# Two groups of key blocks per value burst in the attention heads, and block scores between the query products

## The chip, the cores and the metric

The program runs on one core of one Trainium2 chip. The metric is the device time of one execution in microseconds (us), the median of several runs. The engines are TensorE (PE for its matmuls, PEld for its weight loads), VectorE (DVE), ScalarE (ACT), GpSimd (POOL), and SyncE (SP), which issues most transfers. Each engine works through its own queue in order. About 0.2% of the time, 3.7 us, is what a measurement of this kernel can tell from no change.

## The reference

Two decoder layers over 512 tokens of width 1024. Each layer is: feed-forward (gated, inner width 2816), normalisation, attention, normalisation, feed-forward, normalisation. The attention of the first layer is a latent attention of 12 heads. The second layer attends to keys and values that are made once from the output of the first, in three branches. Every layer also has four memory heads that attend to a memory of 256 rows; their output stands beside that of the 12 heads in one output projection.

```python
# first layer, 12 heads, causal
s = einsum('bhqd,bhkd->bhqk', qb, k) * scale
p = masked_softmax(s, key_pos <= tq)
o = einsum('bhqk,bhkd->bqhd', p, v)
# second layer: 31 compressed keys, selected blocks, window, each with its gate
s_c = einsum('bghqd,bgnd->bghqn', qb, kc) * scale - m * dist_c
p_c = masked_softmax(s_c, cmp_end <= tq)
o   = gb[..., 0:1] * o_c + gb[..., 1:2] * o_s + gb[..., 2:3] * o_w
# both layers
o_mem = memory_attention(q_mem, mem, w_mem_kv[layer])
mix = concatenate([o_tok, o_mem], -1) @ w_out[layer]
```

With 512 tokens there are 8 blocks of 64, and 16 may be selected, so every block is; the window covers all tokens as well. The selected and the window branch are both a causal attention with a distance bias, over two sets of keys and values.

## The kernel before

Tokens and features are cut into tiles of 128 rows. Products of 32-bit data are made of parts: a value is split into a high and a low part (`split`: one ACT and one DVE instruction), and `mm3` and `feature_major` sum three products of parts. Transposed tiles and the products with values stay plain 32-bit; each such value product appears in the trace as two matmul records.

**The order of the work.** The kernel is written for a framework that takes the instructions in program order, estimates when each would be ready, and lays down a fixed order for each engine; an instruction whose inputs come late may so be placed behind others of its engine that were written after it. Buffers are tiles of pools with a number of slots per tag; a new tile waits until the slot's last reader is done. On chip, each queue is strictly in the order laid down.

**The heads.** `pipeline` (both attentions) walks through the score steps: a head has four, one per query block i = 3, 2, 1, 0. A step issues the score matmuls (L351 to L353 and L883 in the first attention, L1191 and L1193 in the second), a maximum on DVE (L884, L1196), exponentials on ACT (L885, L1198); after two blocks, POOL multiplies the rows with the reciprocal of their sums (L891, L1205) into the tile `pp`. After each score step, one step of `others` (next queries and keys) and one of `all_values` run. When the scores are done, `run_all` goes on with values and the first products of the output projection.

**Values.** The heads' values are done for a pair of heads. `GROUPS_J` cuts the lower triangle of 4 x 4 key and query blocks into three groups: key block 0 with 512 query columns, key block 1 with 384, key blocks 2 and 3 with 256 and 128. The second attention has two branches, so six groups. The schedule `SCHED` is a tuple of steps. The word `a0` is `flipped` for group 0 and the first head of the pair: transposes on PE (L618) into one of two PSUM tiles `tb`, and a copy (L621) on ACT or DVE into a tile `pt`, two slots per head. `b0` is the same for the second head. `x0` is the group's products with the values (L646): per key block one matmul for each head, 64 columns wide, the first head in the lower half of the PSUM tile `o` and the second in the upper half. After the last group, the second attention adds the product with the compressed values (L1220), and `put_mix` splits `o` into the tile that the output projection reads. The last step of a pair and the first step of the next run in the same step of the pipeline. `memory_values` does the same for the two pairs of memory heads (products at L704), one of two key blocks at a time.

**The query products of the second attention.** `nsa_in` makes the gates and memory queries, then six query products (`feature_major`, each 128 features for 512 tokens); `q_out` splits a product into `qf`. Between the first ones run the eight steps of `memory_scores`, in PSUM banks 5 to 7. Then come the scores against the compressed keys: `block_scores` (six matmuls from two entries of `qf`, an ACT copy into `ct`) and `block_softmax` (a load of the bias `al`, four transposes L1069, the softmax L1073 to L1084 on DVE with one ACT exponential), for two of three groups of heads, in iterations 3 to 5; the third group is done later, within the heads. The results are in the tile `pc`, which is transposed and read (L1167) in the heads. `query` issues the loads for a pair's query tiles (L1053 on POOL, L1054 and L1055 on SP). PSUM has eight banks; when the heads begin, the banks 0 to 4 become their score tiles, 5 and 6 the two `tb` tiles and 7 the tile `o`.

Of the kernel before, what the change touches and what calls it, by code (L numbers as in the profile page):

```python
# [9 lines left out]
F32 = mybir.dt.float32  # L10
# [7 lines left out]
P = 128  # L18
T = 512
D = 1024  # L20
NT = 4
# [3 lines left out]
NPAIR = 6  # L25
# [79 lines left out]
def tile_trunk(ctx: ExitStack, tc, a: dict, out):  # L105
    nc = tc.nc
# [70 lines left out]
    def unit(name, idx, look):  # L177
        assert order[W.pos][:2] == (name, tuple(idx)), (order[W.pos], name, idx)
        if W.done <= W.pos:
            prep()  # L180
        ahead(look)
        W.pos += 1
        return W.ready.pop(W.pos - 1)
# [51 lines left out]
    def bank(i):  # L235
        i %= 8
        return (PS.left if i < 5 else PS.right).tile([P, 512], F32, tag=f"b{i}", name="bank")
# [22 lines left out]
    def otile():  # L260
        return PS.right.tile([P, 512], F32, tag="o", name="o")
# [93 lines left out]
    def feature_major(w, ps, c0, c1):  # L355

        hi, lo = w
        if c1 - c0 > 256:
            feature_major(w, ps, c0, c0 + 256)
            feature_major(w, ps, c0 + 256, c1)  # L360
            return
        for k in range(NKT):
            nc.tensor.matmul(ps[:, c0:c1], lhsT=hi[:, k * P:(k + 1) * P], rhs=F.xhi[:, k, c0:c1],  # L363
                             start=k == 0, stop=False)
            nc.tensor.matmul(ps[:, c0:c1], lhsT=hi[:, k * P:(k + 1) * P], rhs=F.xlo[:, k, c0:c1],  # L365
                             start=False, stop=False)
        for k in range(NKT):
            nc.tensor.matmul(ps[:, c0:c1], lhsT=lo[:, k * P:(k + 1) * P], rhs=F.xhi[:, k, c0:c1],  # L368
                             start=False, stop=k == NKT - 1)
# [244 lines left out]
    def flipped(pget, js, par, eng):  # L614

        tb = ttile()
        for c, (j, i) in enumerate(js):
            nc.tensor.transpose(tb[:, c * P:(c + 1) * P], pget(i, j), ident)  # L618
        n = len(js) * P
        pt = F.pt.tile([P, T], F32, tag=f"pt{par}", name="pt", bufs=2)  # L620
        (nc.scalar.copy if eng else nc.vector.tensor_copy)(pt[:, :n], tb[:, :n])  # L621
        return pt
# [70 lines left out]
    def memory_values():  # L693
        for pr in range(2):
            F.o = otile()
            for j in range(2):
                pts = []
                for e in range(2):
                    pts.append(flipped(lambda i, j: F.pm[2 * pr + e][:, i, j * P:(j + 1) * P],
                                       [(j, i) for i in range(NT)], e, e))  # L700
                yield
                for e in range(2):
                    c = 512 + j * 256 + (2 * pr + e) * 64
                    nc.tensor.matmul(F.o[64 * e:64 * e + 64, :], lhsT=F.kv[:, c:c + 64], rhs=pts[e],  # L704
                                     start=j == 0, stop=j == 1)
            put_mix(6 + pr)

# [92 lines left out]
    def mla_heads(cT):  # L800
# [93 lines left out]
        def values(pr):  # L894
# [8 lines left out]

            yield from causal_values(SCHED, 1, pget, v, True, lambda g, e: (g + e) % 2)
            put_mix(pr)

        SCHED = ("a0", "b0", "", "x0 a1", "b1", "x1 a2", "b2", "", "x2")

        def scores():
            yield from memory_scores(lambda n: stile())  # L910
# [146 lines left out]
    def block_scores(g, qf, ps, pool, tag, bufs=1):  # L1057

        for v in range(2):
            mm3(ps, S.kc[:, v, 0], S.kc[:, v, 1], qf[:, 2 * g + v, 0], qf[:, 2 * g + v, 1], v == 0, v == 1)  # L1060
        ct = pool.tile([P, T], F32, tag=tag, name="ct", bufs=bufs)
        nc.scalar.copy(ct, ps)
        return ct

    def block_softmax(pc, g, ct, gt, tb, pool, tag, tp, bufs=1):
        al = pool.tile([P, T], F32, tag=tag, name="al", bufs=bufs)
        nc.sync.dma_start(al, a["alc"][g])
        for i in range(NT):
            nc.tensor.transpose(tb[:, i * P:(i + 1) * P], ct[:, i * P:(i + 1) * P], ident)  # L1069
        sc = pc.rearrange("p t s n -> p (t s) n")  # L1070
        m = tp.tile([P, 16], F32, name="m")
        r = tp.tile([P, NT, 2, 2], F32, name="r")
        nc.vector.tensor_tensor(pc.rearrange("p t s n -> p (t s n)"), tb, al, op=ALU.add)  # L1073
        nc.vector.tensor_reduce(m, sc, axis=AX.X, op=ALU.max, negate=True)
        nc.vector.tensor_tensor(sc, sc, m[:, :, None].to_broadcast([P, 16, 32]), op=ALU.add)
        nc.scalar.activation(pc, pc, AF.Exp)
        rf = r.rearrange("p t v e -> p (t v e)")
        nc.vector.tensor_reduce(rf, sc, axis=AX.X, op=ALU.add)
        gv = gt.rearrange("p t (e h b) -> p t h e b", e=2, h=NPAIR)[:, :, 2 * g:2 * g + 2, :, 0]
        nc.vector.tensor_scalar(rf, rf, 1e-30, None, op0=ALU.max)  # L1080
        nc.vector.tensor_tensor(r, r, gv, op=ALU.mult)
        nc.vector.reciprocal(rf, rf)
        nc.vector.tensor_scalar(rf[:, 0:4], rf[:, 0:4], valid, None, op0=ALU.mult)
        nc.vector.tensor_tensor(sc, sc, rf[:, :, None].to_broadcast([P, 16, 32]), op=ALU.mult)  # L1084

    def nsa_in(gt, qf):
        tst, tp = right_pool("ntmp", 2)
        ws = [unit("wgq", (i,), 5 - i) for i in range(3)]
        wq = [unit("wq", (i,), 2 - i) for i in range(3)]

        def gates_qmem(t):
            ps = bank(t)
            q = slice(t * P, (t + 1) * P)
            for k in range(NKT):
                hi, lo = ws[k // 3]
                c = slice(k % 3 * 292, k % 3 * 292 + 292)
                mm3(ps[:, 0:292], F.xhi[:, k, q], F.xlo[:, k, q], hi[:, c], lo[:, c], k == 0, k == NKT - 1)
            nc.scalar.activation(gt[:, t, :], ps[:, 0:36], AF.Exp, scale=-1.0)
            c = F.xp.tile([P, 256], F32, tag=("g", "b")[t % 2], name="c")
            nc.scalar.copy(c, ps[:, 36:292])  # L1100
            return c

        def qmem(t, c):
            q = slice(t * P, (t + 1) * P)
            pt = bank(4 + t)
            for b in range(2):
                nc.tensor.transpose(pt[:, b * P:(b + 1) * P], c[:, b * P:(b + 1) * P], ident)
            for b in range(2):
                split(F.qm[b][:, 0, q], F.qm[b][:, 1, q], pt[:, b * P:(b + 1) * P], scale=0.125)

        def q_out(i, p):
            split(qf[:, i, 0, :], qf[:, i, 1, :], p, scale=0.125)

        c = [gates_qmem(0), gates_qmem(1)]
        qmem(0, c[0])
        pq = [bank(i) for i in (0, 1, 4)]
        feature_major(wq[0], pq[0], 0, 256)
        qmem(1, c[1])
        for i in (1, 2):
            feature_major(wq[i], pq[i], 0, 256)  # L1120
        c = [gates_qmem(2), gates_qmem(3)]
        qmem(2, c[0])
        late = [c[1]]
        nc.vector.tensor_scalar(gt, gt, 1.0, None, op0=ALU.add)
        scores = memory_scores(lambda n: bank(5 + n % 3))
        for i in range(3):
            feature_major(wq[i], pq[i], 256, 512)
            if late:
                qmem(3, late.pop())
            q_out(i, pq[i])  # L1130
            next(scores)
            next(scores)
        for i in range(3, NPAIR):
            p = bank(i - 1)
            feature_major(unit("wq", (i,), 2), p, 0, T)
            q_out(i, p)
            if i == 3:
                for _ in scores:
                    pass
                F.qx = [[mix_tile(5), mix_tile(4)]]  # L1140
                F.pc = F.mp.tile([P, 2, NT, 4, 32], F32, tag="mx2", name="pc")
                query(0, qf, F.qx[0])
            else:
                block_softmax(F.pc[:, i - 4], i - 4, ct, gt, bank(6), F.xp, f"x{i - 2}", tp)
            if i < 5:
                ct = block_scores(i - 3, qf, bank(5), F.xp, "g")
        tst.close()

    def nsa_heads(gt, qf):
# [58 lines left out]
        def values(pr):  # L1208
# [9 lines left out]

            yield from causal_values(SCHED, 2, pget, v, False, lambda g, e: (g + e) % 2)
            nc.tensor.matmul(F.o, lhsT=S.vc[:, pr % 2], rhs=ptc[:, pr // 2], start=False, stop=True)  # L1220
            put_mix(pr)

        SCHED = ("a0 b0", "a1 x0", "b1 a2", "x1 b2", "x2 a3 b3", "a4 x3", "b4 a5", "x4 b5", "x5")

        def first():
            yield from memory_values()
# [65 lines left out]
    pc = bank(7)  # L1292
# [30 lines left out]
    ast, ap = right_pool("ain0")  # L1323
# [21 lines left out]
    ast, ap = right_pool("ain1")  # L1345
    qf = ap.tile([P, NPAIR, 2, T], F32R, name="qf")
    gt = ap.tile([P, NT, 36], F32, name="gt")
    nsa_in(gt, qf)
    close_f()
    for side in ("left", "right"):  # L1350
# [162 lines left out]
```

## Time and profile before

| what | value |
|---|---|
| median of 3 runs | 1870.72 us (1868.49 to 1872.56) |
| the profiled execution | 1869.39 us, its span 1867.5 us |
| mean granted TensorE clock | 0.997 |
| heads of the first attention, with their start | about 405 to 521 us |
| query products of the second attention | about 1306 to 1347 us |
| heads of the second attention | 1347 to 1483 us |

The rows of the profile have the form "start, duration, engine, line, operation, out<-in, shape, count", with times in us from the start of the span; idle time of the engine ahead of a row, and what ended it, stands in brackets. Consecutive instructions of one line are one row. In a table by windows each engine has its busy time and, in brackets, its instructions; then follow the granted clock of TensorE as a share of full speed, the busy share of the DMA engines and their rate. The rows that carry the argument are shown with the prediction.

### The profile page before, as it was taken

How to read it: one execution, taken by the hardware profiler on the slowest of the kernel's cores; microseconds unless marked ns; L12 is line 12 of the kernel's file. 1: busy time of each engine (PE TensorE's matmuls, PEld its weight loads, DVE VectorE, ACT ScalarE, POOL GpSimd, SP SyncE). 2: the span in 40 equal slices, each digit the busy share in tenths (PEclk: the TensorE clock that was granted, in tenths of full speed). 3: DMA queues.
4: the chain of work that ended last, by engine and by line, in shares of the span. 5: the costliest groups of instructions: out<-in, count | busy, mean ns of one | idle time of the engine just before them, and what ended most of it. 6: DMA issues, size and time to landing. Idle time of an engine off the chain costs nothing.

```text
span 1867.5 us, 31922 instructions
## 1 busy us (share of the span) xinstructions
PE 1842.7 (99%) x12776; PEld 1651.6 (88%) x12776; DVE 1465.6 (78%) x2362; ACT 869.4 (47%) x1435; POOL 164.3 (9%) x185
## 2 busy tenths in 40 slices
PE   9999999999999999999999999999999999999998
PEld 8899899896679899899998998998956689999997
DVE  8798789757668789788897987987677378888887
ACT  6344345456545345334653443444566345434432
POOL 0000000025500000000100000001265100000000
PEclk9999999999999999999999999999999999999999
DMA  6333335531134234234333323343321224323322
GB/s 241 112 114 111 116 105 157 173 102 35 57 113 136 80 102 136 80 102 147 130 127 104 125 91 103 112 138 140 108 46 28 98 77 143 103 90 114 115 81 77
DMA packets 59701, 203.86 MB, mean 109 GB/s; under 512 B 6944, under 2 KB 7216, under 8 KB 59552
## 3 DMA queue, kind: packets, MB, share of 16 engines
q1 hardware_dynamic: 56848, 194.18, 31.8%
q0 software_dynamic: 2416, 7.11, 1.2%
q8 instruction: 101, 1.65, 0.4%
q10 hardware_dynamic: 288, 0.52, 0.1%
q14 instruction: 48, 0.39, 0.1%
HBM read 188.16 MB, written 7.34 MB: 105 GB/s over the span
## 4 chain that ended last, share of the span: by engine, by line
PE 89%; DVE 4%; ACT 2%; issue 2%; POOL 1%; DMA 1%; POOLq 0%; DVEq 0%; ACTq 0%
PE bank L376 13%; PE bank L380 13%; PE bank L377 13%; PE bank L415 4%; PE bank L411 4%; PE bank L413 4%; PE bank L412 4%; PE bank L414 4%; PE bank L416 4%; PE o L646 3%; PE bank L365 3%; PE bank L368 3%; PE bank L363 3%; PE tb L618 3%; PE s L1191 1%
## 5 line engine op out<-in xcount | busy, mean ns | idle before, releaser
L199 ACT CAST whi<-wraw 128x1024 fp32r<-128x1024 f32 (+3 forms) x479 | 463.4, 976 | 547.5 <-PE bank L416 246.9
L200 DVE TENSOR_TENSOR wlo<-wraw,whi 128x1024 fp32r<-128x1024 f32 (+3 forms) x479 | 536.4, 1126 | 133.7 <-ACT whi L199 132.7
L376 PE MATMUL bank<-t,whi 128*128 128x256 f32 x1232 | 298.4, 278 | 0.0
L377 PE MATMUL bank<-t,whi 128*128 128x256 f32 x1232 | 297.9, 278 | 0.0
L377 PEld LDWEIGHTS bank<-t,whi 128*128 128x128 f32 x1232 | 231.9, 188 | 0.0
L376 PEld LDWEIGHTS bank<-t,whi 128*128 128x128 f32 x1232 | 231.8, 188 | 0.0
L376 PE MATMUL bank<-xhi,whi 128*128 128x256 f32 x924 | 221.9, 277 | 0.0
L377 PE MATMUL bank<-xlo,whi 128*128 128x256 f32 x924 | 221.9, 277 | 0.0
L380 PE MATMUL bank<-t,wlo 128*128 128x256 f32 x1232 | 191.8, 278 | 0.0
L377 PEld LDWEIGHTS bank<-xlo,whi 128*128 128x128 f32 x924 | 173.6, 188 | 0.6
L376 PEld LDWEIGHTS bank<-xhi,whi 128*128 128x128 f32 x924 | 173.6, 188 | 0.6
L380 PEld LDWEIGHTS bank<-t,wlo 128*128 128x128 f32 x1232 | 164.2, 189 | 0.0
L315 DVE SCALAR_TENSOR_TENSOR x<-x,bank 128x512 f32<-128x512 f32 x176 | 112.5, 682 | 58.9 <-PE bank L415 54.4
L380 PE MATMUL bank<-xhi,wlo 128*128 128x256 f32 x924 | 142.9, 277 | 0.0
L363 PE MATMUL bank<-xhi,whi 128*128 128x256 f32 x544 | 130.7, 281 | 1.3 <-ACT xhi L199 1.3
L365 PE MATMUL bank<-xlo,whi 128*128 128x256 f32 x544 | 130.6, 281 | 1.2 <-DVE xlo L200 1.2
L412 PE MATMUL bank<-whi,hhi 128*128 128x512 f32 x336 | 131.0, 390 | 0.0
L414 PE MATMUL bank<-wlo,hhi 128*128 128x512 f32 x336 | 130.9, 390 | 0.0
L411 PE MATMUL bank<-whi,hhi 128*128 128x512 f32 x336 | 130.8, 390 | 0.0
L415 PE MATMUL bank<-whi,hlo 128*128 128x512 f32 x336 | 130.8, 389 | 0.0
L413 PE MATMUL bank<-wlo,hhi 128*128 128x512 f32 x336 | 130.8, 389 | 0.0
L416 PE MATMUL bank<-whi,hlo 128*128 128x512 f32 x336 | 130.7, 389 | 0.0
(330 smaller groups left out, 3542.3 us busy)
## 6 DMA issues: line engine op xcount, KB each, us to landing
wraw<-in_gu SPq DMA_DIRECT2D x175, 512.0 KB, 3.3
wraw<-in_dn SPq DMA_DIRECT2D x88, 512.0 KB, 3.8
wraw<-in_wo SPq DMA_DIRECT2D x16, 512.0 KB, 3.6
wraw<-in_wm SPq DMA_DIRECT2D x8, 512.0 KB, 4.2
x_dram<-x SPq DMA_DIRECT2D x8, 512.0 KB, 2.9
x<-x_dram SPq DMA_DIRECT2D x8, 512.0 KB, 4.5
wraw<-in_w SPq DMA_DIRECT2D x8, 512.0 KB, 4.6
wraw<-in_wq SPq DMA_DIRECT2D x6, 512.0 KB, 3.5
```

The source lines that it names most:

```text
L199: nc.scalar.copy(hi, src)
L200: eng.tensor_tensor(lo, src, hi.bitcast(F32), op=ALU.subtract)
L363: nc.tensor.matmul(ps[:, c0:c1], lhsT=hi[:, k * P:(k + 1) * P], rhs=F.xhi[:, k, c0:c1], start=k == 0, stop=False)
L376: nc.tensor.matmul(ps, lhsT=hi[:, ks], rhs=xh[:, k], start=k == 0, stop=False)
L377: nc.tensor.matmul(ps, lhsT=hi[:, ks], rhs=xl[:, k], start=False, stop=False)
L380: nc.tensor.matmul(ps, lhsT=lo[:, ks], rhs=xh[:, k], start=False, stop=k == 3)
L411: nc.tensor.matmul(p0, lhsT=ahi, rhs=hi[:, 0:512], start=first, stop=False)
L412: nc.tensor.matmul(p1, lhsT=ahi, rhs=hi[:, 512:1024], start=first, stop=False)
L413: nc.tensor.matmul(p0, lhsT=ahi, rhs=lo[:, 0:512], start=False, stop=False)
L414: nc.tensor.matmul(p1, lhsT=ahi, rhs=lo[:, 512:1024], start=False, stop=False)
L415: nc.tensor.matmul(p0, lhsT=alo, rhs=hi[:, 0:512], start=False, stop=last)
L416: nc.tensor.matmul(p1, lhsT=alo, rhs=hi[:, 512:1024], start=False, stop=last)
```

## The change

Three things are changed. In the heads, the steps are ordered so that the groups 0 and 1 are multiplied in one step; in the second attention so are 2 and 3, and 4 and 5. The transposes of the two groups stand in the steps ahead. Each schedule has as many steps as it had.

In the memory values, the transposes of both key blocks come first, in two steps, and then the four products.

In `nsa_in`, the six query products form one loop. The block scores of the first group of heads come ahead of query product 2 and their softmax behind it; those of the second group come ahead of and behind product 4. Both use bank 2. Query products 3, 4 and 5 go to the banks 3, 4 and 5 (before: 2, 3 and 4). The memory scores are spread over the iterations 0 to 3. The tile `pc` has room of its own in the pool of `qf` (4 KB per partition), where before it took over that of a memory key tile.

```diff
@@ memory_values
             F.o = otile()
+            pts = {}
             for j in range(2):
-                pts = []
                 for e in range(2):
-                    pts.append(flipped(lambda i, j: F.pm[2 * pr + e][:, i, j * P:(j + 1) * P],
-                                       [(j, i) for i in range(NT)], e, e))
+                    pts[j, e] = flipped(lambda i, j: F.pm[2 * pr + e][:, i, j * P:(j + 1) * P],
+                                        [(j, i) for i in range(NT)], e, e)
                 yield
+            for j in range(2):
                 for e in range(2):
                     c = 512 + j * 256 + (2 * pr + e) * 64
-                    nc.tensor.matmul(F.o[64 * e:64 * e + 64, :], lhsT=F.kv[:, c:c + 64], rhs=pts[e],
+                    nc.tensor.matmul(F.o[64 * e:64 * e + 64, :], lhsT=F.kv[:, c:c + 64], rhs=pts[j, e],
                                      start=j == 0, stop=j == 1)
             put_mix(6 + pr)
@@ mla_heads
-        SCHED = ("a0", "b0", "", "x0 a1", "b1", "x1 a2", "b2", "", "x2")
+        SCHED = ("a0", "b0", "a1", "b1", "x0 x1", "a2", "b2", "", "x2")
@@ nsa_in
-        for i in range(3):
-            feature_major(wq[i], pq[i], 256, 512)
+        for i in range(NPAIR):
+            if i in (2, 4):
+                ct = block_scores(i // 2 - 1, qf, bank(2), F.xp, "g")
+            if i < 3:
+                feature_major(wq[i], pq[i], 256, 512)
+            else:
+                pq.append(bank(i))
+                feature_major(unit("wq", (i,), 2), pq[i], 0, T)
             if late:
                 qmem(3, late.pop())
             q_out(i, pq[i])
-            next(scores)
-            next(scores)
-        for i in range(3, NPAIR):
-            p = bank(i - 1)
-            feature_major(unit("wq", (i,), 2), p, 0, T)
-            q_out(i, p)
+            if i < 4:
+                next(scores, None)
+                next(scores, None)
+            if i in (2, 4):
+                block_softmax(F.pc[:, i // 2 - 1], i // 2 - 1, ct, gt, bank(2), F.xp, f"x{i // 2 + 1}", tp)
             if i == 3:
-                for _ in scores:
-                    pass
                 F.qx = [[mix_tile(5), mix_tile(4)]]
-                F.pc = F.mp.tile([P, 2, NT, 4, 32], F32, tag="mx2", name="pc")
                 query(0, qf, F.qx[0])
-            else:
-                block_softmax(F.pc[:, i - 4], i - 4, ct, gt, bank(6), F.xp, f"x{i - 2}", tp)
-            if i < 5:
-                ct = block_scores(i - 3, qf, bank(5), F.xp, "g")
@@ nsa_heads
-        SCHED = ("a0 b0", "a1 x0", "b1 a2", "x1 b2", "x2 a3 b3", "a4 x3", "b4 a5", "x4 b5", "x5")
+        SCHED = ("a0 b0", "a1 b1", "x0 x1", "a2 b2", "a3 b3", "x2 x3", "a4 b4", "a5 b5", "x4 x5")
@@ tile_trunk
     gt = ap.tile([P, NT, 36], F32, name="gt")
+    F.pc = ap.tile([P, 2, NT, 4, 32], F32, name="pc")
     nsa_in(gt, qf)
```

## The prediction

> **What bounds the kernel now.** I read the page first, then the stages that the change touches as windows, then TensorE's (PE's) order of time in them.
>
> ```profile
> span 1867.5 us, 31922 instructions
> PE 1842.7 (99%) x12776; PEld 1651.6 (88%) x12776; DVE 1465.6 (78%) x2362; ACT 869.4 (47%) x1435; POOL 164.3 (9%) x185
> PE 89%; DVE 4%; ACT 2%; issue 2%; POOL 1%; DMA 1%; POOLq 0%; DVEq 0%; ACTq 0%
> ```
>
> PE is busy 99% of the span and makes 89% of the chain that ended last, so a microsecond taken out of PE's row should come out of the time. But busy counts a matmul that waits inside the array as work. The stages:
>
> ```profile
> core 0: us, PE busy (x) PEld busy (x) DVE busy (x) ACT busy (x) POOL busy (x), PEclk, DMA share, GB/s
> 440.00:480.00 40.00, 40.00 (x229) 26.75 (x227) 30.94 (x71) 25.77 (x71) 24.82 (x31) 1.00 0.09 27
> 1306.00:1347.30 41.30, 40.09 (x327) 38.91 (x326) 21.96 (x38) 19.59 (x54) 9.70 (x8) 1.00 0.38 107
> 1347.30:1370.00 22.70, 19.73 (x110) 12.27 (x111) 20.16 (x35) 14.58 (x45) 11.38 (x10) 1.00 0.27 64
> 1370.00:1374.00 4.00, 4.00 (x15) 1.97 (x14) 0.42 (x1) 3.52 (x14) 0.55 (x1) 0.57 0.46 104
> 1410.00:1455.00 45.00, 44.79 (x263) 27.86 (x262) 31.59 (x65) 30.01 (x97) 23.30 (x21) 1.00 0.09 19
> ```
>
> First attention (440 to 480) and second (1410 to 1455): PE full, DVE and ACT at 65 to 77%. The query products (1306 to 1347): PE 40.09 of 41.3, DVE only 21.96. The first 22.7 us of the second attention are the exception: PE idles 2.97 us while DVE has 20.16. Inside a full stretch:
>
> ```profile
> 1374.85 0.28 PE L1193 MATMUL s<-cbf 128*128 128x256 bf16 x1
> 1374.97 0.49 PE L618 MATMUL tb<-cst,pp 128*128 128x128 f32 x3
> 1375.21 1.19 PE L1191 MATMUL s<-ko,qo 128*128 128x512 f32 x5
> 1376.24 0.28 PE L1193 MATMUL s<-cbf 128*128 128x256 bf16 x1
> 1376.46 0.87 PE L646 MATMUL o<-pt,sv 128*64 128x384 f32 x4
> 1377.25 0.55 PE L618 MATMUL tb<-cst,pp 128*128 128x128 f32 x3
> ```
>
> L646 is the value product: 64 columns per head, the two heads in the two halves of the array (128*64), two records per product. After the same L1193, a transpose starts 0.12 us later (1374.97 - 1374.85), a value burst 0.22 us later: **entering the half-array form costs 0.10 us**. The three transposes after the burst last 0.55 against 0.49: 0.06 more.
>
> **The change, part by part.**
>
> (1) Merged bursts. The cost of leaving the form is seen where two bursts happen to adjoin already:
>
> ```profile
> 1350.14 1.08 PE L704 MATMUL o<-pt,mkv 128*64 128x512 f32 x4
> 1351.15 1.09 PE L618 MATMUL tb<-cst,pm 128*128 128x128 f32 x8
> ...
> 1357.55 1.94 PE L704 MATMUL o<-pt,mkv 128*64 128x512 f32 x8 [0.18 <-DVE mix L200]
> 1359.42 0.66 PE L1167 MATMUL tb<-cst,pc 128*128 128x128 f32 x4
> ```
>
> One burst holds PE 1.01 us to the next start, the double one 1.87 instead of 2.02: 0.15 us saved. With 0.10 for the entry and 0.06 behind it, a merge saves about 0.30 us. Merges: in the second attention six bursts per pair become three, 6 x 3 = 18; in the first three become two, 6; memory values: four become two there, and three (one double, above) become two here, 3 more. 27 x 0.30 = **-8.1 us**. Nothing is added or removed in arithmetic. Lower bound 20 x 0.25 = 5 if some pairs stay apart.
>
> (2) Late second heads. An undisturbed burst lasts:
>
> ```profile
> 1381.64 1.08 PE L646 MATMUL o<-pt,sv 128*64 128x512 f32 x4
> 1474.37 0.87 PE L646 MATMUL o<-pt,sv 128*64 128x256 f32 x8
> ```
>
> and 0.87 for 384 columns (above), so a branch of three is 2.82 us. The same line over both attentions, and the 384-column form in the first (its x1):
>
> ```profile
> 443.00:521.00 78.00, 21.80 (x96) 6.75 (x96) 1.00 0.16 54
> 1364.00:1484.00 120.00, 40.50 (x192) 14.32 (x192) 0.99 0.14 32
> L646 PE MATMUL o<-pt,va 128*64 128x384 f32 x24 | 9.5, 512 | 0.0
> ```
>
> First attention: 21.80 - 6 x 2.82 = 4.9 us too long; second: 40.50 - 12 x 2.82 = 6.7, of which I put 2.0 down to the first pair (an estimate: its x0 lies across the stretch at clock 0.57 above), so 4.7. In those bursts the second head's copy was not there, and the halves ran after each other. The first attention's x1 holds 9.5 - 6 x 0.87 = 4.3 of its 4.9: it follows b1 by one step. After the change x1 starts behind x0, about 1.0 us of PE work later, and x0, x2, x4 of the second attention get a whole step more. I take all 4.3 and half of the other 5.3, **-6.9 us**; bounds 0 (the waits move to the transposes) and -9.6.
>
> (3) Start of the second attention.
>
> ```profile
> 1345.79 0.60 PE L1069 MATMUL bank<-cst,ct 128*128 128x128 f32 x4
> 1347.27 0.85 PE L618 MATMUL tb<-cst,pm 128*128 128x128 f32 x6 [0.87 <-DVE pc L1073]
> ...
> 1362.39 0.63 PE L618 MATMUL tb<-cst,pp 128*128 128x128 f32 x4 [0.32 <-ACT ptc L1168]
> 1363.43 1.21 PE L1191 MATMUL s<-ke,qe 128*128 128x512 f32 x4 [0.42 <-ACT pp L1198]
> ...
> 1368.76 0.33 PE L618 MATMUL tb<-cst,pp 128*128 128x128 f32 x1 [1.38 <-POOL pp L1205]
> 1369.76 0.63 PE L618 MATMUL tb<-cst,pp 128*128 128x128 f32 x3 [0.67 <-POOL pp L1205]
> 1346.40:1357.00 10.60, 0.00 (x0) 0.00 (x0) 4.19 (x5) 0.63 (x1) 1.00 0.47 114
> ```
>
> The last row is the tile pc alone: the second block softmax puts 4.19 us of DVE work into a stage where DVE is the fullest engine. Moved ahead of query product 5 it meets a DVE with 41.3 - 21.96 = 19 us free in the query stage. PE's waits of 2.97 us (the four from 1362 on and the 0.18) hang on the head softmax behind it, and after the last two PE's clock is 0.57 over 4 us, 1.7 us lost. Of 4.7 us I take **-2.0**; bounds 0 and -4.7. The Trainium skill, "TensorE: Matmul & The Clock Gate", section "Why this matters for your kernels", warns of idle gaps above some 3 us; here 1.38 and 0.67 close together sufficed, so by the page the 1.7 would not be at stake, and the sum would move by under 1 us.
>
> (4) The boundary. The 0.87 us wait for L1073 goes. What is late next is query product 5, now in bank 5, which the first transpose tile may take over:
>
> ```profile
> 1345.99 0.60 ACT L202 ACTIVATE qf<-bank 128x512 fp32r<-128x512 f32 x1 [2.62 <-PE bank L368]
> 1347.04 0.68 DVE L203 SCALAR_TENSOR_TENSOR qf<-bank,qf 128x512 fp32r<-128x512 f32 x1
> ```
>
> 0.60 + 0.68 us from the product's end. If the transposes are queued ahead of the first score product, PE waits 1.3 us there; if behind, nothing. Bounds -0.87 and +0.45; I take 0.
>
> (5) What moves along. Each block step issues six score matmuls, an ACT copy, four transposes, nine DVE and one ACT instruction, and one load on SP; POOL gets nothing, its query loads keep their place.
>
> ```profile
> 1291.40 0.33 SPq L1067 DMA_DIRECT2D al<-in_alc  x1
> 1301.69 0.33 SPq L1067 DMA_DIRECT2D al<-in_alc  x1
> L1073 DVE TENSOR_TENSOR pc<-bank,al x2: 684/687/690, 1340.6 to 1346.4; 128x512 f32<-128x512 f32 x2
> ```
>
> The loads are issued 40 us ahead of their use, ahead of the query loads already: 0. PE may wait for a split query or for ct, and the head-of-line DVE chain delays the memory score maxima behind it: +0.5 (bounds 0 and 2).
>
> (6) New waits among the transposes. The two transpose tiles are now filled in adjoining steps at three places per pair, 18 in all: the second set waits for the copies of the first.
>
> ```profile
> 1396.79 0.55 PE L618 MATMUL tb<-cst,pp 128*128 128x128 f32 x3
> 1397.43 0.48 ACT L621 COPY pt<-tb 128x384 f32<-128x384 f32 x1 [0.40 <-PE tb L618]
> 1349.42 1.22 DVE L1196 TENSOR_REDUCE nm<-s 128x2 f32<-128x1024 f32 x1
> PE tb L618 <- DVE pt L621: 0.6, 2, 0.4
> ```
>
> A copy is done 0.57 us after its transposes if its engine is free (the 1.22 us maximum is what may stand ahead of it); before, such neighbours (two places per pair) cost 0.6 us in the whole stage. So between 0.9 and 18 x 0.57 = 10.3 us: I take +2.5, nearer the wait that was seen. In the last pair no score products stand between; three places at about 0.6 make +1.5 (bounds 0 and 3).
>
> **Sum**: -8.1 - 6.9 - 2.0 + 0 + 0.5 + 2.5 + 1.5 = -12.5 us. The profiled execution took 1869.4 us (span 1867.5), 1.3 below the median of 1870.7 and inside the runs' 1868.5 to 1872.6, so I take the sum off the median: **1858.2 us**.
>
> **The rivals.**
>
> *All of it, no new waits.* -8.1 - 9.6 - 4.7 + 0.5 = -22: 1849. For it: the stages are PE's alone. Against: the order is made anew for everything.
>
> *The late copies move.* Merges hold, but the second heads' copies make the transposes wait instead: part 2 is 0, -8.1 - 2.0 + 4.5 = -5.6: 1865. For it: DVE copies behind maxima of 1.22 us. Against: x1 has 1 us more in any case.
>
> *It doesn't do what it says.* The planner that orders instructions split some bursts before, and may place score products between x0 and x1. With 10 merges and half of part 2: -3.0 - 4.8 - 1.0 + 4.5 = -4.3: 1866.4.
>
> *Slower.* The engines that empty PSUM become the bound: at the 18 places of part 6 the copy stands behind a DVE maximum, 0.57 + 1.22 us, less 1.03 of score products between (1375.21 to 1376.24): 0.76 each, 13.7 us; with the tail's 1.5 and the merges, and nothing from parts 2 and 3, +7.1: 1877.8. It turns slower than before once a place costs over (8.1 - 1.5) / 18 = 0.37 us with part 2 gone. Against it: two such places per pair cost 0.6 us in all. The Trainium skill, "TensorEngine Tiling (Array Packing)", section "PSUM Bottleneck", states this rule: a tiled PE gains nothing where the copies out of PSUM bind. By the stage row they do not on average: DVE 31.59 of 45.
>
> **How the numbers follow.** Chances: forecast 0.57, all of it 0.09, copies move 0.16, split order 0.10, slower 0.08. About 0.2% (3.7 us) is what a measurement can tell from no change. Faster: 0.57 + 0.09 + 0.12 + 0.05 = 0.83 (the third and fourth lie close to the bound); same 0.04 + 0.05 + 0.01 = 0.10; slower 0.07. The range goes from all of it to just past the split order, 1849 to 1867, leaving 0.04 below and 0.16 above.
>
> **What would show it.** Right: L646 bursts of 8 and 12 records with no other PE row inside, three per pair in the second attention; L646 busy in the two attentions down from 62.3 us to some 52; no wait for L1073 at 1347; PEclk 1.00 after the first pair. Wrong: L646 rows still in fours, or PE waits on pt L621 of many microseconds; a wait for qf L203 of 1.3 us at the boundary; a longer query stage.

## The result and the profile after

The changed kernel takes 1857.77 us (median of 4 runs, 1857.36 to 1858.64), the kernel before 1871.45 beside it (4 runs, 1868.49 to 1872.56). The ratio is 0.9932, 95% interval 0.9919 to 0.9946, which is 12.7 us of 1871.45. The prediction was 1858.2 us. The sum is right; not all of its terms are, as the experiments show.

The totals of the page, and two of the stages that the prediction showed, now of the changed kernel (engines and columns as there). Its second attention begins at 1341.55, with its first score product, where that of before began at 1347.3 with transposes; the windows are placed by that:

```profile
span 1855.6 us, 31915 instructions
PE 1833.6 (99%) x12776; PEld 1652.6 (89%) x12776; DVE 1463.0 (79%) x2362; ACT 869.6 (47%) x1435; POOL 162.6 (9%) x185
```

```profile
1300.25:1341.55 41.30, 40.47 (x333) 39.67 (x331) 24.02 (x43) 19.51 (x54) 10.02 (x8) 1.00 0.37 102
1341.55:1364.25 22.70, 20.32 (x113) 12.40 (x111) 17.11 (x30) 16.72 (x52) 10.70 (x11) 1.00 0.32 73
```

PE has as many matmuls as before and is 9.1 us less busy (1842.7 - 1833.6), which is most of the 11.9 us by which the span is shorter. In the first 22.7 us of the second attention DVE has 17.11 us for 20.16, since the block softmax has moved into the query stage ahead of it (24.02 for 21.96). Yet PE idles 2.38 us of those 22.7 and 0.33 right behind them, hardly less than before (2.97).

The value products L646 alone, over both attentions, and three bursts of a pair of the second, each with the row that follows it:

```profile
443.00:521.00 78.00, 17.21 (x96) 6.35 (x96) 1.00 0.23 77
1358.00:1474.00 116.00, 33.54 (x192) 12.90 (x192) 0.99 0.16 36
```

```profile
1424.95 1.72 PE L646 MATMUL o<-pt,sv 128*64 128x512 f32 x8
1426.60 0.96 PE L1190 MATMUL s<-ko,mix 128*128 128x512 f32 x4
...
1430.24 1.81 PE L646 MATMUL o<-pt,sv 128*64 128x256 f32 x12
1431.98 1.20 PE L1190 MATMUL s<-ke,qe 128*128 128x512 f32 x4
...
1435.99 1.52 PE L646 MATMUL o<-pt,sv 128*64 128x384 f32 x12
1437.44 1.13 PE L1219 MATMUL o<-ptc,svc 128*128 128x512 f32 x2
```

L646 is busy for 50.75 us where it was 62.30; the prediction's mark was some 52. This pair has three bursts, of 8, 12 and 12 records, with nothing between their records; so have four of the six pairs, while in the first and the third PE was given other products between. The bursts shown hold PE for 1.65, 1.74 and 1.45 us (start to the next start). A burst is here a run of L646 records with no other matmul between; over both attentions there are 37 of them, where there were 60.

PE's waits from 1300 to 1480 (engine, tile and line, what ended the wait: us in total, times, longest), and the boundary:

```profile
PE tb L618 <- POOL pp L1204: 2.2, 2, 1.9
PE s L1190 <- ACT pp L1197: 1.0, 2, 0.5
PE bank L352 <- DVE qf L203: 0.8, 1, 0.8
PE tb L618 <- DVE pt L621: 0.3, 1, 0.3
```

```profile
1341.55 1.07 PE L1190 MATMUL s<-ke,mix 128*128 128x512 f32 x4
...
1345.89 2.96 PE L705 MATMUL o<-pt,mkv 128*64 128x512 f32 x8
...
1352.10 1.94 PE L705 MATMUL o<-pt,mkv 128*64 128x512 f32 x8
```

The wait for pc L1073 is gone. The heads begin with score products at 1341.55, not with transposes, so nothing waits for bank 5. The waits on copies into pt, of which the prediction feared 4 us, are 0.3 us. The wait on POOL's scaled rows stays.

To see where PE's time went, each matmul is charged with the time from its start to the next start on PE, less idle time; sums over both attentions (first: from its first transpose to its last value product; second: from its first score product to its last L1219, L1220 before). They are worked out from the trace of one execution each; the two versions named schedules and apart are experiments below.

| us on PE | before | schedules alone | after | apart |
|---|---|---|---|---|
| value products, first attention | 20.15 | 16.11 | 16.10 | 16.50 |
| transposes L618, first | 15.45 | 14.45 | 14.56 | 14.83 |
| idle, first | 2.36 | 2.44 | 0.55 | 0.56 |
| value products, second | 37.79 | 31.08 | 31.86 | 34.23 |
| transposes L618, second | 29.50 | 28.32 | 28.33 | 29.90 |
| idle, second | 3.75 | 4.62 | 3.86 | 5.60 |
| memory value products, both | 7.93 | 7.93 | 9.64 | 9.64 |
| both attentions in all | 242.58 | 230.20 | 231.73 | 238.64 |

Value products and their transposes fell by 12.0 us (102.89 to 90.85). That is about the whole gain. Some 1 us of it is the clock, not the order: in the executions traced for before, after and apart a few us of the second attention ran at a granted clock of 0.57, and before these lay on a value burst. The trace of e1_first, whose second attention has the schedule of before and no such stretch, gives 36.89 and 29.22 us where the table has 37.79 and 29.50 for before, 1.2 less. The execution traced for schedules alone has none either:

```profile
1347.00:1370.00 23.00, 19.96 (x109) 11.90 (x107) 17.89 (x34) 16.03 (x55) 14.09 (x13) 1.00 0.25 56
```

### The profile page after: what moved, and what is told of

The parts are those of the page before. It is cut to its first block, busy times and chain, and to the rows that moved or that the text cites. A ratio compares the mean times of both kernels' runs of the same rounds, so it can differ in the third digit from the quotient of the medians.

```text
span 1855.6 us, 31915 instructions
## 1 busy us (share of the span) xinstructions
PE 1833.6 (99%) x12776; PEld 1652.6 (89%) x12776; DVE 1463.0 (79%) x2362; ACT 869.6 (47%) x1435; POOL 162.6 (9%) x185
## 3 DMA queue, kind: packets, MB, share of 16 engines
q8 instruction: 101, 1.65, 0.4%
## 4 chain that ended last, share of the span: by engine, by line
PE 92%; DVE 4%; ACT 2%; issue 1%; POOL 1%; DMA 0%; POOLq 0%; DVEq 0%; ACTq 0%
PE bank L376 13%; PE bank L380 13%; PE bank L377 13%; PE bank L411 5%; PE bank L412 5%; PE bank L413 5%; PE bank L414 5%; PE bank L415 5%; PE bank L416 5%; PE bank L365 3%; PE bank L368 3%; PE bank L363 3%; PE tb L618 2%; PE o L646 2%; PE s L1190 1%; PE bank L352 1%
```

## The experiments

The theory is that of the prediction: the schedules save by merged bursts and by copies that come in time, and the start of the second attention saves some 2 us more. Rivals are told with each run. Times stand beside those of the kernel before, measured together with them.

### The schedule of the first attention alone (e1_first)

```diff
-        SCHED = ("a0", "b0", "", "x0 a1", "b1", "x1 a2", "b2", "", "x2")
+        SCHED = ("a0", "b0", "a1", "b1", "x0 x1", "a2", "b2", "", "x2")
```

> The kernel before with the new schedule of the first attention alone. Theory M+L (a merge of two value bursts saves 0.30 us, and second heads that came late no longer hold the array): six merges are 1.8 us, the late second heads 4.3 us, together about -5.5 us; the value products' busy time in that attention falls from 21.80 to about 17.2 us. Rival (merges alone count): -1.8 us. Rival (the wait moves): the value line is shorter, but the transposes wait instead and the time stays within 1 us.

Measured: 1863.7 us, before 1869.5; ratio 0.9971 (0.9960 to 0.9982), 5.8 us less by the medians. The 384-column products of its x1 had 9.5 us before; the groups by form now give:

```profile
L646 PE MATMUL o<-pt,va 128*64 128x384 f32 x24 | 6.1, 490 | 0.0
```

3.4 of the 4.3 us went with the longer lead and the merge. What a late copy does is seen in one x1 of the kernel before, on PE and on DVE:

```profile
448.12 1.49 PE L646 MATMUL o<-pt,va 128*64 128x384 f32 x4
448.16 0.55 DVE L621 COPY pt<-tb 128x384 f32<-128x384 f32 x1
```

The second head's copy ends at 448.71, 0.59 us after the burst has begun. In the trace the first head's two records start at 448.12 and 448.50, the second head's at 448.76 and 449.13: the halves run one after the other, 1.49 us for 0.87. Where both copies are there, as in the burst at 1381.64, the records of the two heads start within 0.01 us of each other.

### The schedule of the second attention alone (e2_second)

```diff
-        SCHED = ("a0 b0", "a1 x0", "b1 a2", "x1 b2", "x2 a3 b3", "a4 x3", "b4 a5", "x4 b5", "x5")
+        SCHED = ("a0 b0", "a1 b1", "x0 x1", "a2 b2", "a3 b3", "x2 x3", "a4 b4", "a5 b5", "x4 x5")
```

> The kernel before with the new schedule of the second attention alone. Theory M+L: some 15 realised merges at 0.30 and 4 us of late second heads, about -7 us, less new waits. If the move of the block softmax is needed for the gain (VectorE is full at the start of this attention), only -3 to -4 us. The half-clock stretch at the start stays in either case.

Measured: 1861.33 us, before 1869.5; 0.9959 (0.9946 to 0.9971), 8.2 us less by the medians. L646 in the second attention takes what it takes in the full change:

```profile
1358.00:1484.00 126.00, 33.58 (x192) 12.91 (x192) 0.99 0.18 51
```

### The query products alone (e3_query)

Both schedules and `memory_values` are those of before.

```diff
+        for i in range(NPAIR):
+            if i in (2, 4):
+                ct = block_scores(i // 2 - 1, qf, bank(2), F.xp, "g")
...
+            if i in (2, 4):
+                block_softmax(F.pc[:, i // 2 - 1], i // 2 - 1, ct, gt, bank(2), F.xp, f"x{i // 2 + 1}", tp)
...
+    F.pc = ap.tile([P, 2, NT, 4, 32], F32, name="pc")
```

> The kernel before with the block scores and their softmax moved between the query products, and nothing else. As predicted (part 3: the start of the second attention waits for the softmax on VectorE): the 0.87 us wait goes, the idle time of 2.97 us behind it falls by a half or more, about -2 to -3 us. Rival (the start hangs on GpSimd's multiplications of the second head, not on the softmax): the boundary wait goes, some 0.8 to 1.4 us, and the waits for GpSimd and the half-clock stretch stay.

Measured: 1870.28 us, before 1869.5; 1.0004 (0.9996 to 1.0013). The move by itself brings nothing that can be measured. The first 22.7 us of its second attention, which begins at 1345.42, and PE's longest wait there:

```profile
1345.40:1368.10 22.70, 20.14 (x111) 12.18 (x110) 17.67 (x31) 15.96 (x50) 10.33 (x11) 1.00 0.32 73
```

```profile
PE tb L618 <- POOL pp L1203: 1.7, 2, 1.4
```

DVE has 2.5 us less to do there than before (17.67 for 20.16), and the wait for POOL's rows, 1.38 + 0.67 us before, is 1.7. So the greater part of it does not come from DVE being full. The 0.87 us at the boundary went too, but new waits stand against it: 0.8 us for qf L203 in the query products, 0.5 more for pp L1196 and 0.3 for a copy. What the wait for POOL hangs on is seen on DVE and POOL of the same kernel:

```profile
1365.04 1.34 DVE L1170 SCALAR_TENSOR_TENSOR rs<-rs,gt 128x4 f32<-128x4 f32 x1
1366.30 0.68 DVE L1194 TENSOR_REDUCE nm<-s 128x2 f32<-128x512 f32 x1
1366.90 0.16 DVE L1171 RECIPROCAL rs<-rs 128x4 f32<-128x4 f32 x1
```

```profile
1363.04 3.32 POOL L1203 TENSOR_TENSOR pp<-pp,rs 128x768 f32<-128x768 f32 x2 [1.09 <-ACT pp L1196]
1367.20 1.61 POOL L1203 TENSOR_TENSOR pp<-pp,rs 128x256 f32<-128x256 f32 x2 [0.85 <-DVE rs L1171]
```

L1170 works on four elements per partition and lasts 1.34 us. It ends at 1366.38, where POOL's two multiplications of the head's first two blocks end (1363.04 + 3.32 = 1366.36). The reciprocal comes behind it and behind one maximum (0.68), and only then can POOL scale the last two blocks, for which PE waits.

### The memory values alone (e4_memory)

The part of the diff in `memory_values`, its core:

```diff
                 yield
+            for j in range(2):
                 for e in range(2):
                     c = 512 + j * 256 + (2 * pr + e) * 64
-                    nc.tensor.matmul(F.o[64 * e:64 * e + 64, :], lhsT=F.kv[:, c:c + 64], rhs=pts[e],
+                    nc.tensor.matmul(F.o[64 * e:64 * e + 64, :], lhsT=F.kv[:, c:c + 64], rhs=pts[j, e],
```

> The kernel before with the memory values alone: both key blocks transposed, then four products. Three merges at 0.30 us make -0.9 us; not to be told from no change by the time, so the number of value bursts at L705 in the trace and the time from the first to the last of them decide. Rival: the products wait for the fourth copy, and it is 0 or slower.

Measured: 1868.46 us, before 1869.5; 0.9992 (0.9984 to 1.0001). The part of the merges that lies here, forecast at 0.9 us, is not to be told from nothing by the time. The trace tells: L705 has seven bursts, as many as before. In the first attention one pair's two bursts became one of eight records, but those of the other became three, since the order laid down on chip puts other products between them:

```profile
418.03 1.07 PE L705 MATMUL o<-pt,mkv 128*64 128x512 f32 x2
...
419.70 1.08 PE L705 MATMUL o<-pt,mkv 128*64 128x512 f32 x4
...
421.21 1.07 PE L705 MATMUL o<-pt,mkv 128*64 128x512 f32 x2
```

So no burst was saved here, and the memory value products hold PE 0.84 us longer than before (by the accounting of the table). Against that, two waits of the first attention of the kernel before are gone:

```profile
PE s L353 <- POOL qt L200: 1.1, 1, 1.1
PE s L353 <- DVE qt L200: 0.8, 1, 0.8
```

Every version with this part of the diff lacks them, and before, e1, e2, e3, e10 and e12, without it, have them. The changed kernel has six bursts, and its products hold PE longest (9.64 for 7.93 in the table). There the eight records of the first pair of the second attention do adjoin, but the last two wait for the fourth copy, which ACT ends at 1347.73: 2.96 us by the row at 1345.89 against 1.94 for the second pair.

### Both schedules and nothing else (e10_schedules)

Edit: the two diffs of e1 and e2 together.

> The kernel before with both new schedules, without the changes to memory values and query products. If those two are worth nothing (alone they measured 0.9992 and 1.0004 of before): as fast as the changed kernel, within 2 us, around 1857. If the moved softmax adds its 2 us once the heads are faster: 2 us slower.

Measured: 1857.89 us, before 1870.25; 0.9933 (0.9921 to 0.9945). This is the whole gain of the change, within the intervals. The two other parts, together, are worth nothing that can be measured.

### The same lead without the merges (e5_apart)

```diff
-        SCHED = ("a0", "b0", "a1", "b1", "x0 x1", "a2", "b2", "", "x2")
+        SCHED = ("a0", "b0", "a1", "b1", "x0", "x1 a2", "b2", "", "x2")
-        SCHED = ("a0 b0", "a1 b1", "x0 x1", "a2 b2", "a3 b3", "x2 x3", "a4 b4", "a5 b5", "x4 x5")
+        SCHED = ("a0 b0", "a1 b1", "x0", "x1 a2 b2", "a3 b3", "x2", "x3 a4 b4", "a5 b5", "x4 x5")
```

The lines are against the changed kernel. x0 and x1 (x2 and x3 too) stand in steps of their own, with the transposes as far ahead as in the changed kernel or further: by the schedule 18 of the 24 merges of the heads are undone.

> The changed kernel with the groups' transposes as early as in it, but x0 and x1 in steps of their own (in the second attention x2 and x3 too; x4 and x5 stay together): a group's copies have a step more, and the bursts are apart. Theory M+L: the late second heads stay gone, but 18 merges are given back at 0.30 us: 5.4 us slower than the changed kernel (about 1863). If only the lateness counted: as fast as the changed kernel, 1857.8. If only the merges counted: 12 us slower, near the kernel before.

Measured: 1863.22 us, before 1870.25; 0.9966 (0.9952 to 0.9979): 5.4 us more than the changed kernel by the medians (5.2 to 6.4 by its two ratios, 0.9938 and 0.9932), where 18 x 0.30 was forecast. The table of PE's time splits it: value products +2.77 and transposes +1.84, 4.6 us; idle +1.75, which is waiting for copies that this order brings, so not all of the 5.4 is the price of the form. On chip some of the steps adjoin again: the trace has 51 bursts for 37, so 14 merges were undone and not 18, and the 4.6 us are 0.33 for each. The waits:

```profile
PE tb L618 <- DVE pt L621: 1.6, 3, 0.8
PE tb L618 <- ACT pt L621: 0.9, 2, 0.4
```

### Three groups per burst (e7_three)

Against the changed kernel: three slots for `pt`, and one burst for each branch.

```diff
-        pt = F.pt.tile([P, T], F32, tag=f"pt{par}", name="pt", bufs=2)
+        pt = F.pt.tile([P, T], F32, tag=f"pt{par}", name="pt", bufs=3)
-        SCHED = ("a0", "b0", "a1", "b1", "x0 x1", "a2", "b2", "", "x2")
+        SCHED = ("a0", "b0", "a1", "b1", "a2", "b2", "", "", "x0 x1 x2")
-        SCHED = ("a0 b0", "a1 b1", "x0 x1", "a2 b2", "a3 b3", "x2 x3", "a4 b4", "a5 b5", "x4 x5")
+        SCHED = ("a0 b0", "a1 b1", "a2 b2", "x0 x1 x2", "a3 b3", "a4 b4", "a5 b5", "", "x3 x4 x5")
```

> The changed kernel with all three groups of a branch multiplied in one step and three slots for each copied tile instead of two: in the first attention one burst per pair instead of two, in the second two instead of three. Theory M: 12 merges more at 0.30 us, 3.6 us faster than the changed kernel (about 1854). Rival: the transposes stand in adjoining steps with two PSUM tiles between them, wait for the copies, and take the 3.6 us back or more.

Measured: 1861.05 us, before 1870.25; 0.9950 (0.9938 to 0.9963), 2.2 to 3.4 us more than the changed kernel by its two ratios, whose intervals this one overlaps. The 3.6 us that were expected did not come: merging further does not pay. There are 29 bursts for 37, and yet value products and transposes hold PE 2.0 us longer (by the accounting of the table). In the first attention PE waits anew, most of it for copies:

```profile
PE tb L618 <- DVE pt L621: 1.0, 2, 0.6
```

By the accounting of the table its idle time there is 2.17 us where the changed kernel has 0.55. That is 1.6 us; the rest was not split.

### The second head's rows scaled on VectorE (e8_start, e14_start_again)

Against the changed kernel, for the one head whose rows PE waits for (u = 1). Both runs are of this kernel.

```diff
-                        nc.gpsimd.tensor_tensor(po, po, rs[:, ii, :, None].to_broadcast([P, 2, n]), op=ALU.mult)
+                        (nc.vector if u == 1 else nc.gpsimd).tensor_tensor(po, po, rs[:, ii, :, None].to_broadcast([P, 2, n]), op=ALU.mult)
```

> The changed kernel with the multiplications of the second head of the second attention on VectorE instead of GpSimd. If the start of that attention waits for GpSimd (3.32 us for the first two of them): TensorE's wait of 2.2 us for L1204 goes, and with it the stretch at half clock that follows (1.7 us): 2 to 4 us faster than the changed kernel. If the wait hangs on the chain of scores, maxima and exponentials of that head: it stays, under another name, and the time is the same.

Measured: 1854.15 us, before 1870.25; 0.9916 (0.9903 to 0.9930). The wait has only changed its name:

```profile
PE tb L618 <- DVE pp L1204: 1.7, 1, 1.7
```

```profile
1357.86 2.08 DVE L1204 TENSOR_TENSOR pp<-pp,rs 128x768 f32<-128x768 f32 x2
1359.86 0.15 DVE L1171 SCALAR_TENSOR_TENSOR rs<-rs,gt 128x4 f32<-128x4 f32 x1
1359.94 1.22 DVE L1195 TENSOR_REDUCE nm<-s 128x2 f32<-128x1024 f32 x1
1361.07 0.16 DVE L1172 RECIPROCAL rs<-rs 128x4 f32<-128x4 f32 x1
1361.16 0.92 DVE L1195 TENSOR_REDUCE nm<-s 128x2 f32<-128x768 f32 x1
1362.00 1.01 DVE L1204 TENSOR_TENSOR pp<-pp,rs 128x256 f32<-128x256 f32 x2
```

Without POOL beside it the same instruction on four elements lasts 0.15 us. But the multiplications stand in DVE's own queue, 2.08 us ahead of it, a maximum of 1.22 us stands ahead of the reciprocal, and the last two blocks wait behind another of 0.92 us between the reciprocal and them. PE still waits 1.7 us. A DVE order without these maxima was not tried.

> The kernel of e8_start again, with five rounds. If the second head's scaling on VectorE is worth something, the ratio to before is again about 0.9916, some 3 us below the changed kernel's 0.9932 (about 1855 against 1858 beside a kernel before of 1870.5). If it is worth nothing, as the version without the other moves (e12_best, 0.994) said, the ratio is 0.993 to 0.994 and the first result was the scatter of one call.

Measured: 1855.73 us, before 1870.66; 0.9926 (0.9912 to 0.9940), between the two values expected. The intervals of both runs overlap those of the changed kernel, so a gain of 1 to 3 us is possible, and not shown.

### The first pair's values two steps later (e11_late_start)

```diff
-            yield from paced(10, first())
+            yield from paced(12, first())
```

> The changed kernel with the values of the second attention begun two score steps later. The wait for the second head's scaled rows (1.7 to 2.2 us under either engine) hangs on that head's own chain of scores, maxima and exponentials: two steps are some 4 us of score products, so the wait goes and with it a possible stretch at half clock; against it, two steps more stand at the end with fewer products between. Theory: -2 to -4 us against the changed kernel of the same call, less 1 for the end. Rival: the end takes all of it back, 0.

Measured: 1862.14 us, before 1868.04; 0.9968 (0.9955 to 0.9980), some 6 us slower than the changed kernel measured beside it (e13, below). The wait for POOL is there as before:

```profile
1361.74 0.96 PE L1190 MATMUL s<-ke,qe 128*128 128x512 f32 x4
...
1364.69 0.70 PE L618 MATMUL tb<-cst,pp 128*128 128x128 f32 x3 [1.87 <-POOL pp L1204]
```

But the edit did not do what it was meant to do. These rows have the same order as in the changed kernel, where the same four score products start at 1360.62 and the transposes at 1363.59, after a wait of 1.89 us: on chip the transposes stand behind the same products, not two steps later. So whether the wait goes when they come later was not tested. What did change lies behind it. Copies are late in new places:

```profile
PE tb L618 <- DVE pt L621: 1.2, 3, 0.7
```

By the same accounting as in the table, value products in the second attention hold 34.62 us, not 31.86, though there are 22 bursts for 24; some of 12 records hold PE 2.1 to 2.65 us where the changed kernel has 1.74 to 1.86. So the copies have lost part of their lead. Which placement did it was not traced.

### Both schedules with the second head on VectorE (e12_best), and the changed kernel again (e13_after)

The first is e10 with the edit of e8; the second has no edit.

> The kernel before with both new schedules and the second head's multiplications on VectorE; memory values and query products as before. If these two parts of the change are worth nothing in time: as fast as the run with the multiplications on VectorE alone (ratio 0.9916 of before); and 0 to 3 us below the changed kernel of the same call.

> The changed kernel again, beside the other two of this call: ratio 0.993 of before, as when it was first measured. It gives the bound within which e11 and e12 can be told from it.

Measured: e12 1856.87 us, 0.9940 (0.9927 to 0.9952); e13 1856.24 us, 0.9938 (0.9924 to 0.9952); before 1868.04. e12 stands where the two schedules without the edit stood (0.9933), so the edit of e8 brings nothing that can be measured to the schedules alone. No version here is shown to beat the change.

## Why the prediction was right, and where it was not

**(1) Merged bursts: right.** Most of the bursts are those foretold, 23 fewer than before where 24 were forecast in the heads, and undoing 14 of them cost 5.4 us; by the trace 4.6, or 0.33 each, stand in the products and transposes themselves, and 0.30 was forecast. That the whole 5.4 is 18 x 0.30 is luck. The merges of the memory values are the exception: of their 0.9 us none was seen. Alone (e4) they did not come about on chip, and in the changed kernel one of them waits for its fourth copy.

**(2) Late second heads: right, in the place where it was put.** The x1 of the first attention gave 3.4 of the 4.3 us. The prediction says of these matmuls that they wait inside the array; the rows under e1 show that the second head's half stands empty while the first head's products run. For the second attention no run separates copies in time from fewer bursts. Parts 1 and 2 without the memory values were forecast at 24 x 0.30 + 6.9 = 14.1 us; value products and transposes show 12.0 in the changed kernel and 12.9 with the schedules alone, some 1 us of both being the stretch at clock 0.57.

**(6) New waits among transposes: far too dear.** Forecast 2.5 + 1.5 us; the waits on pt in the second attention are 0.3 us, less than the 0.6 of before. PE's idle time over both attentions did not rise in the changed kernel (6.11 to 4.41 us; the 1.9 us of waits for qt that went with the memory values are in this), and rose by 0.95 in e10. The forecast took a wait at 18 places. What stands at such a place of the changed kernel:

```profile
1427.53 0.82 PE L618 MATMUL tb<-cst,pp 128*128 128x128 f32 x6
1428.10 0.71 PE L1190 MATMUL s<-ko,mix 128*128 128x512 f32 x2
...
1428.97 1.09 PE L618 MATMUL tb<-cst,pp 128*128 128x128 f32 x8
```

Score products stand between two sets of transposes for 0.87 us (1428.97 - 1428.10), longer than the 0.57 us of a copy. In e7, where more transposes stand in adjoining steps, such waits come.

**(3) Start of the second attention: wrong.** Forecast -2.0, measured nothing: e3 is at 1.0004, and e10 without the move is as fast as the whole change. The step that failed is "hang on the head softmax behind it": the wait was put down to the block softmax's 4.19 us on a full DVE. DVE was freed of it, and the wait on POOL went from 2.05 to 2.2 us; the sign "PEclk 1.00 after the first pair" failed with it in this execution (0.57, see the last section). The rows of the changed kernel, DVE first:

```profile
1360.27 1.54 DVE L1171 SCALAR_TENSOR_TENSOR rs<-rs,gt 128x4 f32<-128x4 f32 x1
1361.73 0.68 DVE L1195 TENSOR_REDUCE nm<-s 128x2 f32<-128x512 f32 x1
1362.33 0.16 DVE L1172 RECIPROCAL rs<-rs 128x4 f32<-128x4 f32 x1
```

```profile
1358.47 3.32 POOL L1204 TENSOR_TENSOR pp<-pp,rs 128x768 f32<-128x768 f32 x2 [0.91 <-ACT pp L1197]
1362.93 1.61 POOL L1204 TENSOR_TENSOR pp<-pp,rs 128x256 f32<-128x256 f32 x2 [1.14 <-DVE rs L1172]
```

```profile
1363.59 0.55 PE L618 MATMUL tb<-cst,pp 128*128 128x128 f32 x3 [1.89 <-POOL pp L1204]
```

Read from the bottom: PE waits for POOL, POOL for the reciprocal, the reciprocal for a small DVE instruction that ends when POOL's first two multiplications end (1360.27 + 1.54 = 1361.81; 1358.47 + 3.32 = 1361.79). The first head's rows are hidden behind memory work; the second's are not, and by these rows their own chain of scores, exponentials and scaling sets the time. Taking 2.5 us (e3) or 3 us of other work from DVE took at most 0.35 us from the wait.

**(4) The boundary: 0 was right in sum.** The wait of 0.87 us went and bank 5 cost nothing, as the scores were put first. But the memory values took about as much: 2.96 us for the first burst, 1.0 over the undisturbed one.

**(5) What moves along: right in size.** One wait of 0.8 us for a split query (qf L203) in the first block scores; forecast 0.5.

So the sum of 12.5 came out by luck, because two errors met: (3) with the memory merges and (5), -2.0 - 0.9 + 0.5, gave nothing, 2.4 us less than forecast, while the schedules, forecast at -14.1 + 4.0 = -10.1, gave -12.4 in e10. Of the rivals, the slower one and the one in which late copies move fell on the same row: copies make PE wait 0.3 us, not 0.76 in each of 18 places. The one with a split order, in which 10 merges are left, fell with 23 bursts fewer, and all of it with the waits that stayed at the start of the second attention.

Open: whether the edit of e8 is worth 1 to 3 us; whether the wait at the start goes if the transposes do come later; and how the gain of the second attention divides between fewer bursts and earlier copies. The first attention has 1.8 us less idle time in the changed kernel than in e1 and e10. That comes with the memory values, whose edit alone (e4) shows it too; it does not show in the medians, the memory products being 1.7 us longer.

## What to carry to other kernels

A product in half the array has a price at both ends of a burst, here some 0.3 us in all, so gather such products; but only as far as their inputs are there, since a burst waits for its last copy. What a second input's lateness costs stands in the matmul rows, where no view of waits shows it: compare the busy time of a form with what its undisturbed bursts would take (9.5 us against 6 x 0.87). Count the bursts in the trace and not in the schedule, since another order may be laid down on chip. And when a wait is named after an engine, follow its chain to the end before work is taken off a busy engine on its behalf: here a four-element instruction ended only with two multiplications of 3.32 us, the next two waited for what came behind it, and 2.5 to 3 us of other work taken from DVE brought nothing in time.

## What the runs showed of the hardware

**A small VectorE instruction ended only with GpSimd's.** The rows above show it in e3 and after: 1.34 and 1.54 us for four elements per partition, ending within 0.02 us of POOL's multiplications, and 0.15 us in e8, where POOL has none there. The Trainium skill, "SBUF — State Buffer", section "Who interferes with whom", says that a DVE instruction with two SBUF inputs and a GpSimd instruction that reads SBUF exclude each other for the whole instruction; the trace agrees.

**After the same gaps the granted clock fell in one execution and not in another.** Over the same 4 us, in the changed kernel's first profiled execution and in that of e13, the same program:

```profile
1364.00:1368.00 4.00, 3.67 (x15) 2.68 (x14) 1.14 (x3) 2.37 (x9) 1.08 (x2) 0.57 0.40 82
```

```profile
1364.00:1368.00 4.00, 4.00 (x20) 2.35 (x20) 2.88 (x7) 2.71 (x10) 1.97 (x3) 1.00 0.49 104
```

PE's waits ahead of it are 1.89 and 0.33 us in the one and 1.90 and 0.33 in the other. At 0.57 of full speed 4 us lose 1.7 us of PE's work, so that the 1.7 us which part (3) counted was never the kernel's to win for sure. The Trainium skill, "TensorE: Matmul & The Clock Gate", section "What's actually happening", calls the window of 3413 ns free-running and its effect different from run to run; these two executions agree with that.
